# Order of the long and short products in the gate and up units, and the place of one norm's spread

## The chip, the cores and the metric

The kernel runs on one core of one Trainium2 chip. The metric is the device time of one execution in microseconds; the time before is the median of three runs. TensorE (PE) multiplies, VectorE (DVE) and ScalarE (ACT) split the weights and empty PSUM, GpSimd (POOL) does small side work, and SyncE (SP) issues the transfers.

## The reference

256 tokens of width 1024 go through two layers. Each has a half-step SwiGLU block, a mixer (a Mamba-2 scan in the first layer, sliding-window attention in the second) and a second half-step SwiGLU block; a final norm ends it. All is float32. A SwiGLU block, of which there are four, is the part that the change touches:

```
def swiglu(h, w_gate, w_up, w_down):
    return (jax.nn.silu(h @ w_gate) * (h @ w_up)) @ w_down
x = x + FFN_RES_WEIGHT * swiglu(rmsnorm(x, norm_w[layer, 0]), ffn_w_gate[layer, 0], ffn_w_up[layer, 0], ffn_w_down[layer, 0])
```

The inner width is 2816, which is 22 tiles of 128.

## The kernel before

Weights come as units of 128 by 1024, in the order of a list that the program fixes. A unit is split into a rounded part `hi` (ACT, L145) and the rest `lo` (DVE, L156), four units ahead of its use (`ahead`). The activations are split in the same way into `xh` and `xl`, which lie side by side in a tile `xs` of 512 columns for each of the eight slices k of the width. A product of two split numbers needs three of the four parts: hi times xh, hi times xl, lo times xh.

The four SwiGLU blocks have the keys f0 to f3. For each tile f of the inner width a block has a gate unit g, an up unit u and, from f = 4 on, a down unit d of the tile four earlier. The last down units follow at the block's end.

A gate or up unit (`wide`, L357) has 16 matmuls into one PSUM bank: eight **long products** of 512 columns (hi times xs, which is xh and xl at once) and eight **short products** of 256 columns (lo times xh, into the bank's first half). With f = 0 long and short ones alternate, since the activations of slice k become ready one by one. With f > 0 all eight long products come first and then all eight short ones. A down unit (`rows`, L379) has 24 matmuls of 256 columns. After the products ACT copies the bank's second half and DVE adds the first half (`add`, L516).

The normalizing factor of a block is not applied to the input but to the results. `rs_slots` (L418) spreads this work over the units: `h0` sums the squares on PE (L312), and after it DVE and POOL take the root; `h1` builds a diagonal matrix on DVE (L332); `h2`, the **spread**, multiplies it on PE (L337), and ACT copies the factors `rs` out (L339). What may run behind a unit stands in a table of slots, one slot for each unit; `tick` runs it when the unit's matmuls have been issued. In f0 `h0` stands in slot 3, `h1` in slot 4 and `h2` in slot 5, which is behind the up unit of f = 2. In the other blocks they stand in slots 0, 1 and 2, so that `h2` is behind the gate unit of f = 1.

When `rs` is there, `evac` turns g and u of a tile into the split operand of the down unit in three steps, one slot apart: e0 scales (L494, L496) and applies silu, e1 multiplies (L499) and rounds to `hh`, e2 takes the rest `hl` (L503). In f0 the results of the first tiles wait for `rs`; the line that holds them back is

```
wait = max(0, 5 - f) if key == "f0" else 2 if f == 0 else 0
```

Each engine runs its instructions in the order in which the program issues them.

Of the kernel before, what the change touches and what calls it, by code (L numbers as in the profile page):

```python
# [18 lines left out]
D = 1024  # L19
KT = D // P  # L20
# [10 lines left out]
DI = 2048  # L31
HEADS = 32
GROUPS = 4
# [183 lines left out]
class Trunk:  # L217
# [138 lines left out]
            before()  # L356
        self.tick()  # L357

    def wide(self, what, out, by_part=False):


        hi, lo = self.W.next(what)
        passes = [(k, w, x, n) for k in range(KT) for w, x, n in ((hi, self.xs, 2 * T), (lo, self.xh, T))]
        if by_part:
            passes = passes[0::2] + passes[1::2]
        for n, (k, w, x, c) in enumerate(passes):
            self.nc.tensor.matmul(  # L367
                out[:, 0:c], w[:, k * P : (k + 1) * P], x[k],
                start=n == 0, stop=n == len(passes) - 1, skip_group_check=True,
            )  # L370
        self.tick()
# [43 lines left out]

        return done

    def rs_slots(self, acc, n, key, d, got, quick=False):  # L418

        st = {}  # L420

        def h0():
            st["b"], st["y"] = self.rs_stats(acc(), n, key)

        def h1():
            st["dg"] = self.rs_diag(st["y"], key)

        def h2():
            got(self.rs_spread(st["b"], st["dg"], key), st["y"])

        self.slots.late(d, h0)
        self.slots.at(d + 1, h1)
        self.slots.late(d + (1 if quick else 2), h2)

    def last_stage(self):
        nc = self.nc
# [38 lines left out]
    def stage_norm(self, key):  # L475
        def got(rs, y):
            self.rs, self.rtok = rs, y

        self.rs_slots(lambda: self.sq_parts, D, key, 3 if key == "f0" else 0, got)


    def ffn(self, l, i, key, nxt):
        nc, wk = self.nc, self.fw
        self.stage_norm(key)
        accs = self.accs(f"da_{key}")
        hs = {}

        def evac(f, g, u):
            hh = self.op.tile([P, T], F32R, tag="high", name=f"hh_{key}_{f}")
            hl = self.op.tile([P, T], F32R, tag="low", name=f"hl_{key}_{f}")  # L490
            hs[f] = (hh, hl)

            def e0():
                nc.vector.tensor_tensor(g, g, self.rs, ALU.mult)  # L494
                nc.scalar.activation(g, g, AF.Silu)
                nc.vector.tensor_tensor(u, u, self.rs, ALU.mult)  # L496

            def e1():
                nc.vector.tensor_tensor(u, u, g, ALU.mult)  # L499
                nc.scalar.activation(hh, u, AF.Copy)  # L500

            def e2():
                nc.vector.tensor_tensor(hl, u, hh.bitcast(F32), ALU.subtract)  # L503

            wait = max(0, 5 - f) if key == "f0" else 2 if f == 0 else 0
            self.slots.chain(wait, [e0, e1, e2])

        def product(name, f, t):

            b = self.bank(f"{name}_{key}_{f}")  # L510
            if self.W.pos == 0:
                self.slots.at(0, lambda: nc.scalar.copy(t, b[:, 0:T]))
                self.unit((name, l, i, f), b[:, 0:T])
                return

            def add():  # L516
                nc.scalar.copy(t, b[:, T:])  # L517
                nc.vector.tensor_tensor(t, b[:, 0:T], t, ALU.add)  # L518

            self.slots.at(0, add)  # L520
            self.wide((name, l, i, f), b, by_part=f > 0)

        for f in range(NF):
            g, u = (wk.tile([P, T], F32, tag=n, bufs=4, name=f"{n}s_{key}_{f}") for n in "gu")
            product("g", f, g)
            evac_now = lambda: evac(f, g, u)
            self.slots.late(0, evac_now)
            product("u", f, u)
            if l == 1 and i == 0 and f == 0:
                self.split_k()  # L530
            if l == 1 and i == 0 and f == 5:
                self.shared_k()
            if f >= LAG:
                self.down(l, i, f - LAG, hs, accs)
        for f in range(NF - LAG, NF - TAIL):
            self.down(l, i, f, hs, accs)
        self.tail([(("d", l, i, f), *hs.pop(f)) for f in range(NF - TAIL, NF)], accs, nxt)
# [15 lines left out]
    def ssm(self, nxt):  # L553
# [19 lines left out]
        yh, yl, sq, R = {}, {}, {}, {}  # L573
# [92 lines left out]
        def csb(hg):  # L666
            t = wk.tile([P, 4, 3 * P], F32, tag="csb", bufs=2, name=f"csb{hg}")
            nc.sync.dma_start(t, scratch[4 * hg : 4 * hg + 4, :].unsqueeze(0).broadcast_to([P, 4, 3 * P]))
            CSB[hg] = t

        def cb(g):
            b = side(f"cb{g}")
            nc.tensor.matmul(b[:, 0:T], B[g][:, 0:P], C[g], start=True, stop=True)
            nc.tensor.matmul(b[:, T : T + P], B[g][:, P:T], C[g][:, P:T], start=True, stop=True)

            def e():
                m = wk.tile([P, 3, P], F32, tag="cbm", name=f"cbm{g}")
                V.tensor_tensor(m[:, 0], b[:, 0:P], causal, ALU.mult)
                V.tensor_tensor(m[:, 2], b[:, T : T + P], causal, ALU.mult)
                A.copy(m[:, 1], b[:, P:T])  # L680
                CB[g] = m

            sl.at(1, e)
# [22 lines left out]
        def prep(g):  # L706

            es = [wk.tile([P, 2, 3, P], F32, tag="E", bufs=6, name=f"E{4 * g + n}") for n in range(4)]

            def p0(n):  # L710
                tok = st["tok"]
                for i in range(2):
                    h = 8 * g + 2 * n + i
                    row = CSB[h // 4][:, h % 4]
                    A.activation(es[n][:, i, 0:2], row[:, 0:T], AF.Relu, bias=tok[:, 0, h : h + 1])
                    if i == 0:
                        V.tensor_scalar(es[n][:, i, 2], row[:, T:], tok[:, 1, h : h + 1], 0.0, ALU.add, ALU.max)
                    else:
                        A.activation(es[n][:, i, 2], row[:, T:], AF.Relu, bias=tok[:, 1, h : h + 1])

            def p1():
                for e in es:
                    A.activation(e, e, AF.Exp, scale=-1.0)  # L723

            def p2(n):
                f = es[n].rearrange("p n b l -> p n (b l)")
                c = CB[g].rearrange("p b l -> p (b l)").unsqueeze(1).broadcast_to([P, 2, 3 * P])
                V.tensor_tensor(f, f, c, ALU.mult)  # L728
                M[4 * g + n] = es[n]

            sl.chain(0, [lambda: p0(0), lambda: p0(1), lambda: p0(2), lambda: p0(3), p1])
            for n in range(4):
                sl.at(5 + n + DECAY_AT[g], lambda n=n: p2(n))
# [24 lines left out]
        def scale(g):  # L758
            for tt in range(4 * g, 4 * g + 4):
                V.tensor_tensor(ys[tt], ys[tt], R[g], ALU.mult)  # L760
# [36 lines left out]
        for hg in range(8):  # L797
            g = hg // 2
# [5 lines left out]
        for g in range(GROUPS):  # L804
            plan(E["C", g] + 3 + SLACK, lambda g=g: cb(g))
            sl.at(base + start[g] - sl.now, lambda g=g: prep(g))
            for hg in (2 * g, 2 * g + 1):
                y = ymm_at[hg]
                plan(turned[hg], lambda hg=hg: xtok(hg))
                plan(start[g] - 2 + 2 * (hg % 2), lambda hg=hg: csb(hg))  # L810
                plan(y, lambda hg=hg: ymm(hg))
            last = max(max(ymm_at[t // 2] + 1, E["z", t] + 2) for t in range(4 * g, 4 * g + 4))

            def got(rs, y, g=g):
                R[g] = rs

            def norm(g=g, got=got):
                self.rs_slots(lambda: sq[g], DI // GROUPS, f"yg{g}", 0, got, True)

            plan(last + 1 + NORM_AT[g], norm)  # L820
            done = last + 3 + NORM_AT[g] + SCALE_AT[g]
            sl.at(base + done - sl.now, lambda g=g: scale(g))
            for tt in range(4 * g, 4 * g + 4):
                n = min(at["so", tt], NIN - TAIL) - 3
                if n < done:
                    n = min(at["so", tt], NIN - TAIL) - 2
                assert n >= done, (tt, n, done)
                sl.at(base + n - sl.now, lambda tt=tt: ysplit(tt))
# [414 lines left out]
```

## Time and profile before

| | |
|---|---|
| median of three runs | 1035.71 us (1035.37, 1035.71, 2038.25) |
| the profiled execution's own time | 1036.34 us |
| its span | 1034.5 us |
| mean granted TensorE clock | 0.997 |
| PE busy | 1014.0 us, 98% of the span |
| DVE busy | 780.1 us, 75% |
| ACT busy | 627.9 us, 61% |
| POOL busy | 80.4 us, 8% |

One run of the three took 2038.25 us, twice the others; the median stands beside the two that agree. The span is counted from the first to the last instruction, and 1.8 us of the profiled execution's time lie around it. The busy time of PE is an envelope: matmuls overlap in the pipeline, each shows 0.28 or 0.39 us, and the distance between two starts is shorter. Distances between starts are what is read below.

### The profile page before, as it was taken

What the parts mean: (1) busy time and instruction counts of PE and PEld (TensorE: products, weight loads), DVE (VectorE), ACT (ScalarE), POOL (GpSimd) and SP (SyncE); (2) the same over time, 40 slices, a digit from 0 to 9 for tenths busy, and PEclk for the clock granted to TensorE, in tenths of its full rate; (3) what the DMA queues carried; (4) which work ended last, traced back from release to release, by engine and by line L of the source; (5) the groups of instructions that cost most, each with busy time, mean ns of one, the idle gap of its engine ahead of it and who ended that gap; (6) DMA issues with size and microseconds to landing.
All of it is one profiled execution on the core that took longest, in us unless ns stands there. A gap on an engine that the chain in (4) does not pass through costs nothing.

```text
span 1034.5 us, 18344 instructions
## 1 busy us (share of the span) xinstructions
PE 1014.0 (98%) x7290; PEld 940.7 (91%) x7290; DVE 780.1 (75%) x1418; ACT 627.9 (61%) x1106; POOL 80.4 (8%) x124
## 2 busy tenths in 40 slices
PE   9999999999999999999999999999999999999996
PEld 8899999999989898999999899999998898999996
DVE  5866666889999978766667896666689877666665
ACT  7555555669886756555555664555565775555554
POOL 3000000210111112000000200000022020000000
PEclk9999999999999999999999999999999999999998
DMA  8555554556546354555555465555545335555531
GB/s 327 206 182 201 192 195 180 176 188 264 184 150 225 132 194 173 190 196 204 173 202 202 157 208 206 171 203 197 199 175 161 117 132 201 187 180 204 188 118 41
DMA packets 29845, 190.85 MB, mean 184 GB/s; under 512 B 3744, under 2 KB 5312, under 8 KB 8256
## 3 DMA queue, kind: packets, MB, share of 16 engines
q1 hardware_dynamic: 29328, 188.90, 51.3%
q8 instruction: 57, 0.93, 0.4%
q10 hardware_dynamic: 432, 0.79, 0.2%
q14 instruction: 28, 0.23, 0.1%
HBM read 187.27 MB, written 1.10 MB: 182 GB/s over the span
## 4 chain that ended last, share of the span: by engine, by line
PE 82%; DVE 9%; ACT 4%; DMA 2%; POOL 2%; issue 1%; POOLq 0%; SPq 0%
PE da_f L387 23%; PE u_f L367 23%; PE g_f L367 23%; PE sa L387 4%; PE sb L354 3%; DVE lo L156 2%; DMA csb<-cs_scratch 2%; PE aa L387 2%; PE q L354 1%; DVE xs L606 1%; ACT hi L145 1%; DVE E L728 1%; ACT E L723 1%; PE kab L354 1%; DMA X<-x 1%
## 5 line engine op out<-in xcount | busy, mean ns | idle before, releaser
L156 DVE TENSOR_TENSOR lo<-raw,hi 128x1024 fp32r<-128x1024 f32 (+1 forms) x343 | 414.7, 1213 | 11.7 <-ACT hi L145 11.7
L145 ACT ACTIVATE hi<-raw 128x1024 fp32r<-128x1024 f32 (+1 forms) x343 | 356.8, 1047 | 10.3 <-PE sa L387 4.3
L387 PE MATMUL da_f<-hh_f,lo 128*128 128x256 f32 x704 | 195.0, 277 | 0.0
L387 PE MATMUL da_f<-hh_f,hi 128*128 128x256 f32 x704 | 194.9, 277 | 0.0
L387 PE MATMUL da_f<-hl_f,hi 128*128 128x256 f32 x704 | 194.9, 277 | 0.0
L367 PE MATMUL u_f<-xs,hi 128*128 128x512 f32 x704 | 179.9, 393 | 0.0
L367 PE MATMUL g_f<-xs,hi 128*128 128x512 f32 x696 | 176.9, 393 | 0.3 <-DVE xs L399 0.3
L367 PEld LDWEIGHTS u_f<-xs,hi 128*128 128x128 f32 x704 | 126.5, 188 | 22.2
L367 PEld LDWEIGHTS g_f<-xs,hi 128*128 128x128 f32 x696 | 124.6, 188 | 23.3 <-DVE xs L399 1.1
L387 PEld LDWEIGHTS da_f<-hl_f,hi 128*128 128x128 f32 x704 | 132.2, 188 | 0.0
L387 PEld LDWEIGHTS da_f<-hh_f,lo 128*128 128x128 f32 x704 | 132.2, 188 | 0.0
L387 PEld LDWEIGHTS da_f<-hh_f,hi 128*128 128x128 f32 x704 | 132.0, 188 | 0.0
L518 DVE TENSOR_TENSOR gs_f<-g_f,gs_f 128x256 f32<-128x256 f32 x87 | 36.9, 424 | 107.8 <-ACT gs_f L517 107.6
L367 PEld LDWEIGHTS u_f<-xs,lo 128*128 128x128 f32 x704 | 95.3, 188 | 7.1
L367 PEld LDWEIGHTS g_f<-xs,lo 128*128 128x128 f32 x696 | 95.0, 188 | 6.8
L518 DVE TENSOR_TENSOR us_f<-u_f,us_f 128x256 f32<-128x256 f32 x88 | 37.3, 424 | 84.0 <-ACT us_f L517 83.9
L367 PE MATMUL u_f<-xs,lo 128*128 128x256 f32 x704 | 99.7, 277 | 0.0
L367 PE MATMUL g_f<-xs,lo 128*128 128x256 f32 x696 | 99.0, 279 | 0.0
L517 ACT COPY us_f<-u_f 128x256 f32<-128x256 f32 x88 | 32.6, 371 | 106.0 <-PE u_f L367 105.9
L354 PE MATMUL sb<-xs,hi 128*128 128x256 f32 x656 | 86.8, 282 | 0.0
L517 ACT COPY gs_f<-g_f 128x256 f32<-128x256 f32 x87 | 32.1, 369 | 83.1 <-PE g_f L367 83.1
L354 PEld LDWEIGHTS sb<-xs,hi 128*128 128x128 f32 x656 | 80.8, 188 | 0.9 <-issue 0.5
(267 smaller groups left out, 1303.7 us busy)
## 6 DMA issues: line engine op xcount, KB each, us to landing
raw<-w SPq DMA_DIRECT2D x168, 1024.0 KB, 4.9
csb<-cs_scratch SPq DMA_DIRECT2D x8, 768.0 KB, 6.8
raw<-w SPq DMA_DIRECT2D x4, 512.0 KB, 6.8
Q<-r_q SPq DMA_DIRECT2D x32, 32.0 KB, 1.9
out<-o SPq DMA_DIRECT2D x3, 256.0 KB, 2.1
ca<-const_att SPq DMA_DIRECT2D x1, 704.0 KB, 6.3
X<-x SPq DMA_DIRECT2D x2, 256.0 KB, 5.9
first_x<-x SPq DMA_DIRECT2D x1, 288.0 KB, 4.4
```

The costliest lines, as they stand in the source:

```text
L145: self.nc.scalar.activation(hi[:, s], self.chunks[c][:, i, s], AF.Copy)
L156: self.nc.vector.tensor_tensor(lo[:, s], self.chunks[c][:, i, s], hi[:, s].bitcast(F32), ALU.subtract)
L354: nc.tensor.matmul(out, w[:, k * P : (k + 1) * P], x[k], start=n == 0, stop=n == len(passes) - 1)
L367: self.nc.tensor.matmul(out[:, 0:c], w[:, k * P : (k + 1) * P], x[k], start=n == 0, stop=n == len(passes) - 1, skip_group_check=True,)
L387: nc.tensor.matmul(out, w[:, s], x, start=f and j < 4 and m == 0, stop=e and m == 2, skip_group_check=True)
L517: nc.scalar.copy(t, b[:, T:])
L518: nc.vector.tensor_tensor(t, b[:, 0:T], t, ALU.add)
L606: V.scalar_tensor_tensor(out, u[:, tap : tap + T], self.s("convw", tap * 24 + c), out, ALU.mult, ALU.add)
L723: A.activation(e, e, AF.Exp, scale=-1.0)
L728: V.tensor_tensor(f, f, c, ALU.mult)
```

## The change

Three things change. In gate units with f > 0 the eight short products come first and the eight long ones after them. In up units with f > 0 one short product comes first, then the eight long ones, then the other seven short ones. In f0 the spread moves from slot 5 to slot 6, behind the gate unit of f = 3, and the steps of `evac` that wait for it move one slot with it. In the scan's four group norms the argument `True` becomes the gap 1, which is what it meant. No instruction is added or removed.

```diff
-    def wide(self, what, out, by_part=False):
+    def wide(self, what, out, shorts=None):
         hi, lo = self.W.next(what)
         passes = [(k, w, x, n) for k in range(KT) for w, x, n in ((hi, self.xs, 2 * T), (lo, self.xh, T))]
-        if by_part:
-            passes = passes[0::2] + passes[1::2]
+        if shorts is not None:
+            long, short = passes[0::2], passes[1::2]
+            passes = short[:shorts] + long + short[shorts:]
...
-    def rs_slots(self, acc, n, key, d, got, quick=False):
+    def rs_slots(self, acc, n, key, d, got, gap=2):
...
-        self.slots.late(d + (1 if quick else 2), h2)
+        self.slots.late(d + gap, h2)
...
-        self.rs_slots(lambda: self.sq_parts, D, key, 3 if key == "f0" else 0, got)
+        self.rs_slots(lambda: self.sq_parts, D, key, *((3, got, 3) if key == "f0" else (0, got)))
...
-            wait = max(0, 5 - f) if key == "f0" else 2 if f == 0 else 0
+            wait = max(0, 6 - f) if key == "f0" else 2 if f == 0 else 0
...
-            self.wide((name, l, i, f), b, by_part=f > 0)
+            self.wide((name, l, i, f), b, shorts=None if f == 0 else KT if name == "g" else 1)
```

Lines behind the head of `wide` have a number higher by one in the new kernel.

PE, where the gate unit of f = 9 in f0 ends and its up unit begins, before (`xs` with `hi` is a long product, with `lo` a short one):

```order
L367 MATMUL g_f_9_901<-xs_90,lo_807 128x256
L367 MATMUL g_f_9_901<-xs_91,lo_807 128x256
L367 MATMUL u_f_9_927<-xs_84,hi_811 128x512
L367 MATMUL u_f_9_927<-xs_85,hi_811 128x512
L367 MATMUL u_f_9_927<-xs_86,hi_811 128x512
```

The same place in the change:

```order
L368 MATMUL g_f_9_901<-xs_90,hi_779 128x512
L368 MATMUL g_f_9_901<-xs_91,hi_779 128x512
L368 MATMUL u_f_9_927<-xs_84,lo_835 128x256
L368 MATMUL u_f_9_927<-xs_84,hi_811 128x512
L368 MATMUL u_f_9_927<-xs_85,hi_811 128x512
```

The two long groups now lie next to each other, with one short product between them; the gate's short group lies against the down unit before it, and the up unit's last seven against the down unit behind it.

PE, at the spread of f0, before:

```order
L367 MATMUL u_f_2_360<-xs_90,lo_260 128x256
L367 MATMUL u_f_2_360<-xs_91,lo_260 128x256
L337 MATMUL st_f_310<-dg_f_351,ones 128x256
L367 MATMUL g_f_3_392<-xs_84,hi_264 128x512
L367 MATMUL g_f_3_392<-xs_85,hi_264 128x512
```

and in the change:

```order
L368 MATMUL g_f_3_389<-xs_90,hi_264 128x512
L368 MATMUL g_f_3_389<-xs_91,hi_264 128x512
L337 MATMUL st_f_310<-dg_f_351,ones 128x256
L368 MATMUL u_f_3_415<-xs_84,lo_326 128x256
L368 MATMUL u_f_3_415<-xs_84,hi_289 128x512
```

The spread now stands one unit later, behind a gate unit.

DVE, around the rest `hl` of tile 0, which the first down unit of f0 reads, before:

```order
L518 TENSOR_TENSOR us_f_3_391<-u_f_3_418,us_f_3_391 128x256
L156 TENSOR_TENSOR lo_444<-raw_196,hi_416 128x1024
L503 TENSOR_TENSOR hl_f_0_259<-us_f_0_208,hh_f_0_258 128x256
L499 TENSOR_TENSOR us_f_1_267<-us_f_1_267,gs_f_1_266 128x256
L494 TENSOR_TENSOR gs_f_2_332<-gs_f_2_332,rs_f_380 128x256
```

and in the change:

```order
L519 TENSOR_TENSOR gs_f_4_445<-g_f_4_447,gs_f_4_445 128x256
L156 TENSOR_TENSOR lo_471<-raw_262,hi_443 128x1024
L504 TENSOR_TENSOR hl_f_0_259<-us_f_0_208,hh_f_0_258 128x256
L500 TENSOR_TENSOR us_f_1_267<-us_f_1_267,gs_f_1_266 128x256
L495 TENSOR_TENSOR gs_f_2_332<-gs_f_2_332,rs_f_409 128x256
```

`hl` of tile 0 now stands behind the add of the gate unit of f = 4 and not behind that of the up unit of f = 3; the down unit that reads it has kept its place.

## Rows read from the trace of the kernel before

**Rows 1.** Page, part 1: busy time, share of the span, instructions.

```profile
PE 1014.0 (98%) x7290; PEld 940.7 (91%) x7290; DVE 780.1 (75%) x1418; ACT 627.9 (61%) x1106; POOL 80.4 (8%) x124
```

**Rows 2.** Waits of PE, whole span: total us, times, longest.

```profile
PE st_yg L337 <- DVE dg_yg L332: 5.4, 4, 2.0
...
PE st_f L337 <- DVE dg_f L332: 0.5, 1, 0.5
```

**Rows 3.** Timeline, PE, one tile of f0: start, duration, what, count.

```profile
58.91 2.00 PE L367 MATMUL g_f<-xs,hi 128*128 128x512 f32 x8
60.75 1.07 PE L367 MATMUL g_f<-xs,lo 128*128 128x256 f32 x8
61.65 1.99 PE L367 MATMUL u_f<-xs,hi 128*128 128x512 f32 x8
63.48 1.11 PE L367 MATMUL u_f<-xs,lo 128*128 128x256 f32 x8
64.43 0.28 PE L387 MATMUL da_f<-hh_f,hi 128*128 128x256 f32 x1
```

**Rows 4.** Timeline, PE, one tile of f1.

```profile
424.29 1.99 PE L367 MATMUL g_f<-xs,hi 128*128 128x512 f32 x8
426.12 1.11 PE L367 MATMUL g_f<-xs,lo 128*128 128x256 f32 x8
427.06 2.00 PE L367 MATMUL u_f<-xs,hi 128*128 128x512 f32 x8
428.89 1.07 PE L367 MATMUL u_f<-xs,lo 128*128 128x256 f32 x8
429.80 0.28 PE L387 MATMUL da_f<-hh_f,hi 128*128 128x256 f32 x1
```

**Rows 5.** Timeline, PE: first of 120 down products and what follows, f0 and f1.

```profile
181.19 0.28 PE L387 MATMUL da_f<-hh_f,hi 128*128 128x256 f32 x1
...
195.32 0.28 PE L354 MATMUL sb<-xs,hi 128*128 128x256 f32 x1
...
561.53 0.28 PE L387 MATMUL da_f<-hh_f,hi 128*128 128x256 f32 x1
...
575.13 0.39 PE L367 MATMUL g_f<-xs,hi 128*128 128x512 f32 x1
```

**Rows 6.** Timeline, PE, f1, groups of f = 2 and 3 behind the spread.

```profile
405.01 2.00 PE L367 MATMUL g_f<-xs,hi 128*128 128x512 f32 x8
406.86 1.11 PE L367 MATMUL g_f<-xs,lo 128*128 128x256 f32 x8
407.80 2.00 PE L367 MATMUL u_f<-xs,hi 128*128 128x512 f32 x8
409.63 1.07 PE L367 MATMUL u_f<-xs,lo 128*128 128x256 f32 x8
```

**Rows 7.** Timeline, PE, f0, alternating products of the first up unit.

```profile
12.87 0.39 PE L367 MATMUL u_f<-xs,hi 128*128 128x512 f32 x1
13.10 0.28 PE L367 MATMUL u_f<-xs,lo 128*128 128x256 f32 x1
13.22 0.40 PE L367 MATMUL u_f<-xs,hi 128*128 128x512 f32 x1
```

**Rows 8.** Timeline, all engines, the spread of f0, idle time and releaser in brackets.

```profile
27.25 0.48 DVE L332 TENSOR_SCALAR dg_f<-co,y_f 128x128 f32<-128x128 f32 x2 [1.71 <-POOL y_f L325]
...
27.78 0.70 PE L337 MATMUL st_f<-dg_f,ones 128*128 128x256 f32 x2 [0.51 <-DVE dg_f L332]
```

**Rows 9.** Timeline, the rest of tile 0 on DVE and its first reader on PE.

```profile
36.18 0.42 DVE L503 TENSOR_TENSOR hl_f<-us_f,hh_f 128x256 fp32r<-128x256 f32 x1
...
39.52 0.28 PE L387 MATMUL da_f<-hl_f,hi 128*128 128x256 f32 x1
```

**Rows 10.** Timeline, the lower part of the second up unit and that unit's start.

```profile
16.19 1.29 DVE L156 TENSOR_TENSOR lo<-raw,hi 128x1024 fp32r<-128x1024 f32 x1 [2.03 <-ACT hi L145]
...
17.77 0.39 PE L367 MATMUL u_f<-xs,hi 128*128 128x512 f32 x1
```

More of the change, by code (lines that the diff above doesn't have):

```diff
@@ L817, in norm @@
             def norm(g=g, got=got):
-                self.rs_slots(lambda: sq[g], DI // GROUPS, f"yg{g}", 0, got, True)
+                self.rs_slots(lambda: sq[g], DI // GROUPS, f"yg{g}", 0, got, 1)
             plan(last + 1 + NORM_AT[g], norm)
```

## The prediction

> **What bounds the kernel.** I read the shares of busy time first: PE has something in flight for 98% of the span, DVE for 75% [rows 1]. Then the waits of PE: the four spreads of the scan take 5.4 us together, that of f0 0.5 us, and each other group 1.1 us at most; all ten of them come to 11 us of 1034.5 [rows 2]. So the sequence of matmuls sets the time. No other engine can give much, and a reordering can only pay if the same matmuls follow each other faster. I therefore looked in the timeline of PE at the distances between starts, group by group.
>
> One tile of f0 shows it [rows 3]. The gate's eight long products last from 58.91 to 60.75, 1.84 us, its eight short ones 0.90; the up unit's eight long ones 1.83, its short ones 0.95. The short products differ, though shape and operands are alike: 0.90 for the gate, 0.95 for the up unit. In f1 it is the other way round, 0.94 for the gate and 0.91 for up [rows 4]. The down products behind the up unit keep the pace of its short ones. A stretch of 120 of them gives it most sharply: 14.13 us in f0, which is 117.8 ns each, and 13.60 us in f1, 113.3 ns each [rows 5]. So a short product has a **loose** pace and a **tight** one, 4.4 ns apart, and it keeps the pace until a long group comes. A group of eight long products changes it: behind loose ones it ends in tight ones, behind tight ones in loose ones. In the four blocks 82 long groups start behind loose products and end in tight ones, and 74 the other way round. Two groups per tile flip it twice, so a block keeps the foot on which it starts: f0 has its down products loose, f1 to f3 tight.
>
> The exceptions matter. In f1 the gate group at 405.01, the second long group behind the spread, lasts 1.85 us, starts behind loose products and ends in loose ones, 0.94; the next one, 407.80 to 409.63, flips [rows 6]. There are five such groups in the trace.
>
> **The change, part by part.** Nothing is added or removed, so PE, DVE and ACT keep their instructions and the DMA queues their transfers. Five edits remain.
>
> 1. *Order within a tile.* Today 8 short products lie between the two long groups and 32 between tiles. Then 1 lies between the groups and 39 between tiles. If one short product is enough to part two flips, only that one runs loose and 39 run tight. A tile in the steady state: eight short gate products 0.907 (8 x 113.3 ns), long group 1.83, one loose short product 0.118, long group 1.84, seven tight ones 0.793, 24 down products 2.720.
>  - f0: its 22 down units change pace, 528 x 4.4 ns = 2.3 us. Its up units from f = 3 on, 19, go from 0.943 (eight loose) to 0.118 + 0.793 = 0.911: 0.6 us. Its gate groups are tight already. Together **2.9 us**.
>  - f1 to f3: the down products are tight already. 57 gate groups go from 0.943 to 0.907, 2.1 us; 57 up groups from 0.907 to 0.911, -0.2 us. Together **1.9 us**.
>  - The long groups keep their two lengths, 1.83 and 1.84, and only change places: nothing.
>  The first tiles of a block, up to f = 2, and the place in f2 where two key units stand in between have their own pattern before and after; I put them at nothing, and at 0.3 us either way for the range.
>
> 2. *Price of the single short product.* No row shows one between two groups of eight. The nearest are the alternating products of f0's first up unit: a single short product takes 0.12 us (13.10 to 13.22), the long one before it 0.23 [rows 7]. So it costs 0.113 to 0.124 us by itself; I take the loose pace, 0.118. What it does to the next long group those rows don't tell, since there a long product never follows a long one. That is the open point of this case.
>
> 3. *`lo` is wanted at the start of a unit, not in its middle.* It is made four units ahead. The tightest place is the second up unit: its `lo` is done at 16.19 + 1.29 = 17.48, and the unit starts at 17.77 [rows 10]. The new order wants it then and not 1.8 us later; 0.29 us are left, so nothing. If that cover goes, the wait is as long as `lo` is late.
>
> 4. *The spread of f0.* Today PE stands for 0.51 us because the diagonal starts on DVE only at 27.25 [rows 8]. One unit later it has been ready for 2 us: **0.5 us** saved. The copy of `rs` is then late by one unit, and with it the whole chain on DVE. Queued behind it there are the adds and the `lo` parts, but these have units to spare. The first down unit has not: `hl` of tile 0 ends at 36.60, and its reader starts at 39.52 [rows 9]. From the spread to that end it takes 36.60 - 27.78 = 8.82 us. The new spread comes after 27.27 (no wait) plus one gate unit of 2.76: 30.03. So `hl` ends at about 38.85, and its reader is due at 39.52 - 0.51 = 39.01. 0.16 us remain: nothing, or up to 0.4 us if DVE is held up once more.
>
> 5. *The results leave PSUM as before*: the copy waits for a unit's last product in either order, and a unit has the same 16.
>
> The sum: 2.9 + 1.9 + 0.5 = 5.3 us off the profiled execution's 1036.34, which is 1031.0. That execution is 0.6 us above the median of 1035.71, and a median is what will be measured, so the forecast is 1035.7 - 5.3 = **1030.4**. Its own range is 1029.6 to 1031.7: 0.3 us down and 0.3 + 0.4 + 0.6 up, for what I put at nothing and for the base. The rivals too are given against the median.
>
> [...] The same shape runs at 113.3 and at 117.8 ns, by what ran before it [rows 5]. [...]
>
> **The rivals.**
>
> *Order is worth nothing.* If the pace depends on the block and not on the order, only edit 4 counts: 1035.7 - 0.5 = 1035.2. Against it: gate and up have opposite paces in the same block, and swap them between f0 and f1 [rows 3, 4]. Chance 0.1.
>
> *Flips, but on the wrong foot.* Two flips per tile keep what the block starts with. If the products behind the spread leave the 39 loose and the one tight: the down products of f1 to f3, 3 x 528 x 4.4 ns = 7.0 us, their 57 up groups 0.030 each = 1.7, the gate groups of f0 19 x 0.037 = 0.7, less 0.5: +8.9, **1044.6**. For it: in f1 the first groups behind the spread are loose for three units before the pattern settles [rows 6]. Against it: it settles on the tight foot in three blocks whose spread stands behind a gate unit, where f0's will stand too. Chance 0.15.
>
> *No flip behind a single product: slower than before.* The second of two long groups parted by one short product may be like the one at 405.01, which lasted 1.85 and left the pace loose [rows 6]. Then all 40 short products of a tile are loose and nothing brings the tight pace back: 7.0 for the down products, 57 up groups 2.1, f0's gate groups 0.7, long groups 0.01 each for 152, 1.5, less 0.5: +10.8, **1046.5**. It decides as soon as one loose product does not count as a loose group. For it: all 82 flips had 8 or more short products before them, and the flip has a count of its own, as the five exceptions show. Against it: the exceptions all follow a disturbance of the stream, the spread or foreign units, and behind a lone short product the long ones of [rows 7] last as long as others. Chance 0.2.
>
> *Block by block.* One or two blocks on the wrong foot: each costs about 3.5 us in f1 to f3 (a third of 7.0 + 1.7, and the 0.6 us of its gain), so 1033.9 to 1037.4. Chance 0.05.
>
> **The numbers.** The forecast has 0.5: 82 of 87 long groups behind loose products flipped. The range runs from 1029.6, the lower end of the forecast, to 1047.0. It holds the forecast, the first, second and last rival, together 0.8, and the lower side of the third, whose long groups could cost a little more than the 0.01 us set here. The two signs share most of the chance; the forecast's own range is 1029.6 to 1031.7. About 2% is what a measurement of this kernel is taken to tell from no change; that is 20.7 us. No case reaches that: faster 0.01, within 2% 0.97, slower 0.02 for a wait that I don't see.
>
> **What the changed profile would show.** Right: a tile takes 8.21 us in all four blocks (0.907 + 1.83 + 0.118 + 1.84 + 0.793 + 2.720), before 8.34 in f0 and 8.23 in f1; 120 down products at a block's end last 13.6 us in f0 too; the spread of f0 has no wait on DVE; `hl` of tile 0 ends before its reader is due. Wrong: 14.1 us for the 120 in any of f1 to f3 tells of the wrong foot or of no flip. Which of the two, the single short product and the long group behind it tell: with the flip the 39 follow a group of 1.83, without it both long groups leave 118 ns behind them.

## The result, and the profile after

The change took 1044.93 us, median of five runs (1037.92, 1041.96, 1044.93, 1045.0, 1046.38), beside 1035.93 for the kernel before on the same chip: a ratio of 1.0067, 95% interval 1.0054 to 1.0081. The forecast was 1030.4. Its sign was wrong; the time lies within the range and fits the rival *Flips, but on the wrong foot* (1044.6). The five runs lie 8.5 us apart, those of before 1.5 apart but for the one of 2038 us. That scatter is the first clue.

The profiled execution is the 1037.92 one, with a span of 1036.1 us against 1034.5. PE still bounds it, with the same instructions and 3.9 us more busy time than in [rows 1]. First part 1 of its page, then the waits of PE (total us, times, longest).

```profile
PE 1017.9 (98%) x7290; PEld 944.6 (91%) x7290; DVE 780.6 (75%) x1418; ACT 627.9 (61%) x1106; POOL 80.3 (8%) x124
```

```profile
PE st_yg L337 <- DVE dg_yg L332: 3.4, 3, 1.6
```

The wait for the diagonal of f0, 0.5 us in [rows 2], is gone, and no wait in a block has taken its place. The scan's waits fell from 5.4 to 3.4 us, but that gains little: from 296 to 299 us the granted clock was 0.50, sixteen products there took 3.4 us and not 2.0, and they filled time in which PE had waited before. That is also some 1.5 of the 3.9 us of busy time. From the last down product of f0 to the first gate product of f1 it is 196.8 us, against 197.1 before. The loss is pace, not waiting. Here is the timeline of PE in the change (start, duration, what, count), first a tile of f0, which answers to [rows 3], then one of f1, which answers to [rows 4], and the next one of f1 from its gate's long group on.

```profile
57.92 1.07 PE L368 MATMUL g_f<-xs,lo 128*128 128x256 f32 x8
58.83 1.99 PE L368 MATMUL g_f<-xs,hi 128*128 128x512 f32 x8
60.66 0.28 PE L368 MATMUL u_f<-xs,lo 128*128 128x256 f32 x1
60.77 2.01 PE L368 MATMUL u_f<-xs,hi 128*128 128x512 f32 x8
62.62 0.96 PE L368 MATMUL u_f<-xs,lo 128*128 128x256 f32 x7
...
420.83 1.10 PE L368 MATMUL g_f<-xs,lo 128*128 128x256 f32 x8
421.77 2.00 PE L368 MATMUL g_f<-xs,hi 128*128 128x512 f32 x8
423.61 0.28 PE L368 MATMUL u_f<-xs,lo 128*128 128x256 f32 x1
423.73 2.01 PE L368 MATMUL u_f<-xs,hi 128*128 128x512 f32 x8
425.57 0.99 PE L368 MATMUL u_f<-xs,lo 128*128 128x256 f32 x7
...
430.17 2.00 PE L368 MATMUL g_f<-xs,hi 128*128 128x512 f32 x8
432.00 0.28 PE L368 MATMUL u_f<-xs,lo 128*128 128x256 f32 x1
432.11 1.99 PE L368 MATMUL u_f<-xs,hi 128*128 128x512 f32 x8
433.94 0.99 PE L368 MATMUL u_f<-xs,lo 128*128 128x256 f32 x7
```

In f0 the tile is the one that was forecast: eight short products 0.91 (57.92 to 58.83), the long group 1.83, the single short product 0.12, the long group 1.85. In f1 the same eight short ones take 0.94. Two kinds of tile take turns there. In the first nothing flips: both long groups take 1.84, and the single short product between them is as loose as the others (117 ns). In the second the gate's group flips to tight, the single short product is tight (113 ns), and the up unit's group flips back, so that 39 are loose and one is tight. From the first down product of one tile to that of the next it is 8.213 us in f0; in f1 it is 8.395 (no flip) and 8.371 (two flips) in turn. The down products at the end of each block tell the same; these rows are the first of 120 and what follows them, for f0, f1 and f3, and answer to [rows 5].

```profile
178.40 0.28 PE L388 MATMUL da_f<-hh_f,hi 128*128 128x256 f32 x1
...
192.00 0.28 PE L354 MATMUL sb<-xs,hi 128*128 128x256 f32 x1
...
560.53 0.28 PE L388 MATMUL da_f<-hh_f,hi 128*128 128x256 f32 x1
...
574.66 0.40 PE L368 MATMUL g_f<-xs,hi 128*128 128x512 f32 x1
...
1011.44 0.28 PE L388 MATMUL da_f<-hh_f,hi 128*128 128x256 f32 x1
...
1025.05 0.38 PE L457 MATMUL fin<-last_sq,ones 128*128 128x256 f32 x1
```

13.60 us in f0, 14.13 in f1, 13.61 in f3: f0 and f3 run on the tight foot, f1 and f2 on the loose one. Before, f0 was the loose block and the other three were tight. From a block's first down product to its last, before and after:

| | f0 | f1 | f2 | f3 | sum |
|---|---|---|---|---|---|
| before | 155.80 | 153.45 | 159.33 | 153.45 | 622.04 |
| change | 153.29 | 156.54 | 162.30 | 153.11 | 625.24 |

So f0 gained 2.5 us, f3 0.3, and f1 and f2 lost 3.1 and 3.0: a sum of +3.2 us. The rest of the execution, the spread of f0 among it, gave back 1.6; the spans differ by 1.6.

Where do the blocks part? In their first tiles, around the spread. Timeline of PE in the change, the gate's long group before the spread and what follows, of f1 (a block that came out loose) and of f3 (tight):

```profile
396.28 2.01 PE L368 MATMUL g_f<-xs,hi 128*128 128x512 f32 x8
398.13 0.59 PE L337 MATMUL st_f<-dg_f,ones 128*128 128x256 f32 x2
398.37 0.47 PE L368 MATMUL u_f<-xs,lo 128*128 128x256 f32 x1
398.68 2.00 PE L368 MATMUL u_f<-xs,hi 128*128 128x512 f32 x8
400.52 0.99 PE L368 MATMUL u_f<-xs,lo 128*128 128x256 f32 x7
...
850.31 2.00 PE L368 MATMUL g_f<-xs,hi 128*128 128x512 f32 x8
852.15 0.59 PE L337 MATMUL st_f<-dg_f,ones 128*128 128x256 f32 x2
852.39 0.47 PE L368 MATMUL u_f<-xs,lo 128*128 128x256 f32 x1
852.71 2.00 PE L368 MATMUL u_f<-xs,hi 128*128 128x512 f32 x8
854.54 0.96 PE L368 MATMUL u_f<-xs,lo 128*128 128x256 f32 x7
```

The instructions are the same. The short product behind the spread takes 0.31 us in f1 and 0.32 in f3 (306 and 313 ns in the trace's own starts), and the seven behind the long group come out loose in the one and tight in the other, 0.82 and 0.79 us to the next unit. But they differed before the spread: the long group ahead of it takes 1.85 us in f1 and 1.84 in f3, behind eight short products that are loose in both. In the trace's own starts it is 1.851 or 1.852 in all seven loose blocks and 1.838 or 1.839 in all four tight ones, wherever the spread stands behind a gate unit of the new order (the two profiles of the change and that of the order alone, both below). Further ahead lies the block's first tile, whose alternating products wait for slices of the activations one by one; that these waits make the difference is not shown.

The two rows that answer to [rows 8, 9], of the timeline of all engines:

```profile
29.92 0.59 PE L337 MATMUL st_f<-dg_f,ones 128*128 128x256 f32 x2
...
38.16 0.42 DVE L504 TENSOR_TENSOR hl_f<-us_f,hh_f 128x256 fp32r<-128x256 f32 x1
...
38.72 0.30 PE L388 MATMUL da_f<-hl_f,hi 128*128 128x256 f32 x1
```

The spread has no idle time before it. `hl` of tile 0 ends at 38.58; its reader starts 0.14 us later and, at 138 ns behind its predecessor, some 0.02 late. That small wait turns the foot: the rest of this down unit is loose (118 ns), and so are the next tile's gate products (0.94); behind that tile's long groups the products are tight again. In the second profile of the same program the same product comes 140 ns behind its predecessor, and the products stay tight.

### The profile page after: what moved, and what is told of

Read it like the earlier page. It is cut to its first block, busy times and chain, and to the rows that moved or that the text cites. A ratio compares the mean times of both kernels' runs of the same rounds, so it can differ in the third digit from the quotient of the medians.

```text
span 1036.1 us, 18364 instructions
## 1 busy us (share of the span) xinstructions
PE 1017.9 (98%) x7290; PEld 944.6 (91%) x7290; DVE 780.6 (75%) x1418; ACT 627.9 (61%) x1106; POOL 80.3 (8%) x124
## 4 chain that ended last, share of the span: by engine, by line
PE 84%; DVE 9%; ACT 3%; DMA 2%; POOL 1%; issue 1%; POOLq 0%; SPq 0%
PE da_f L388 24%; PE u_f L368 24%; PE g_f L368 23%; PE sa L388 4%; PE sb L354 3%; DVE lo L156 2%; DMA csb<-cs_scratch 2%; PE aa L388 1%; PE q L354 1%; DVE xs L607 1%; DVE E L729 1%; ACT E L724 1%; PE kab L354 1%; DMA X<-x 1%; DVE S L941 1%
## 5 line engine op out<-in xcount | busy, mean ns | idle before, releaser
L368 PE MATMUL u_f<-xs,lo 128*128 128x256 f32 x704 | 114.9, 280 | 0.0
L368 PEld LDWEIGHTS u_f<-xs,lo 128*128 128x128 f32 x704 | 101.9, 188 | 10.4
L368 PEld LDWEIGHTS g_f<-xs,lo 128*128 128x128 f32 x696 | 88.4, 188 | 0.3
```

What stands on the lines that cost most here:

```text
L368: self.nc.tensor.matmul(out[:, 0:c], w[:, k * P : (k + 1) * P], x[k], start=n == 0, stop=n == len(passes) - 1, skip_group_check=True,)
```

## The experiments

The theory after the result: the time goes with the number of blocks on the loose foot (a foot that repeats from tile to tile is also called a course); the order of before comes back to the tight foot after a disturbance, the new order keeps whatever it starts with. Rivals: the foot is fixed by the program; a single short product never parts two flips; the time was lost elsewhere. Every kernel below differs from the change or from another kernel by the lines shown. All times and ratios stand against the kernel before on the same chip: 1037.02 us beside the first four kernels (the two of one part, the two of the switch at f = 4), 1036.1 beside the late switch and two, five and four short products, 1036.18 beside the rest.

**One part each.** The spread moved, the order of before:

```diff
-            self.wide((name, l, i, f), b, shorts=None if f == 0 else KT if name == "g" else 1)
+            self.wide((name, l, i, f), b, shorts=None if f == 0 else 0)
```

> Old order of long and short products in all tiles, only the spread of f0 moved behind the gate unit of f = 3. Theory A (the pace is a state that a block takes on at its start and keeps; the new order has a tight and a loose cycle, the old one only a small difference between its two): f0 now starts as f1 to f3 do, its 22 down units become tight, 2.3 us, and the wait of 0.5 us goes: 1035.9 - 2.8 = 1033.1, all runs within 1 us of each other. Rival B (the moved spread is what disturbs the kernel, by the later factors): 1036 or more, with runs several us apart.

And the new order with the spread in its old place:

```diff
-        self.rs_slots(lambda: self.sq_parts, D, key, *((3, got, 3) if key == "f0" else (0, got)))
+        self.rs_slots(lambda: self.sq_parts, D, key, 3 if key == "f0" else 0, got)
...
-            wait = max(0, 6 - f) if key == "f0" else 2 if f == 0 else 0
+            wait = max(0, 5 - f) if key == "f0" else 2 if f == 0 else 0
```

> New order of products in all four blocks, the spread of f0 in its old slot. Theory A: each block still falls on a tight or a loose foot, about 3.5 us per loose block from 1031: 1031.5 to 1046, several us between runs. Rival B (the moved spread is the cause): about 1031, runs within 1 us.

The spread alone: 1032.86 us (1032.6 to 1034.67, four of the five within 0.4 us), ratio 0.9967, interval 0.9954 to 0.998. The order alone: 1046.01 (1043.25 to 1048.54), 1.0089, 1.0074 to 1.0105; its median is at the upper end of what theory A expected, and its slowest runs lie above. So the whole loss is the order's, and the spread gains 4.2 us, eight times its wait. The rows of the first kernel behind the spread of f0 show where the larger part comes from (timeline of PE):

```profile
29.94 0.59 PE L337 MATMUL st_f<-dg_f,ones 128*128 128x256 f32 x2
...
32.21 1.10 PE L368 MATMUL u_f<-xs,lo 128*128 128x256 f32 x8
...
35.00 1.11 PE L368 MATMUL g_f<-xs,lo 128*128 128x256 f32 x8
...
37.77 1.07 PE L368 MATMUL u_f<-xs,lo 128*128 128x256 f32 x8
```

Two groups behind the spread stay loose (0.95 and 0.94 us for eight short products), the third turns tight. With an up unit next to the spread the third is an up unit, and the down products behind it are tight. Before, a gate unit stood there. In f1 to f3 of the same kernel the three groups are tight, loose, tight (0.91, 0.94, 0.91): another start, and the same foot from the third on. All four blocks of this kernel are tight: 120 down products take 13.60 or 13.61 us in each, and a tile 8.233. From first to last down product f0 takes 153.45 us and not 155.80; that is 2.35 of the 3.7 us between the two profiles' spans. Another 0.7 lie ahead of its first down product, the wait of 0.5 among them, and the rest is spread over the other stages. In the profile of the order alone f1 is tight (8.213) and the other three are loose: not the pair of the change.

**Where the switch comes.** The order of before in a block's first tiles, the new one from f = 4 on:

```diff
-            self.wide((name, l, i, f), b, shorts=None if f == 0 else KT if name == "g" else 1)
+            self.wide((name, l, i, f), b, shorts=None if f == 0 else 0 if f < 4 else KT if name == "g" else 1)
```

> As the change, but f = 1 to 3 of each block keep the old order (long group, then short group); the new order starts at f = 4. Theory A: the three old tiles put every block on the tight foot before the new order starts, and it keeps it: 1030.4, between 1029.6 and 1031.5 in every run; tiles of 8.21 us in all four blocks. Rival C (the new order loses its foot by itself in the course of a block): 1034 to 1046, several us between runs.

1037.61 us (1033.9 to 1039.41), ratio 1.0004, interval 0.9991 to 1.0017: the expected time was missed. Its profile has f1 and f3 tight to their end and f0 loose: there the spread stands right before the switch, within the two groups that stay loose. f2 is tight up to the key units and loose behind them (timeline of PE, f2):

```profile
612.92 0.96 PE L368 MATMUL u_f<-xs,lo 128*128 128x256 f32 x7
613.71 1.12 PE L354 MATMUL kab<-xkh,hi 128*128 128x256 f32 x8
...
627.04 0.98 PE L368 MATMUL u_f<-xs,lo 128*128 128x256 f32 x7
...
630.70 1.10 PE L368 MATMUL g_f<-xs,lo 128*128 128x256 f32 x8
```

So the new order holds the tight foot where nothing disturbs it, and in f2 it does not find it again in the sixteen tiles behind the key units. In the next kernel the gate unit of f = 4 too has the old order, so that the new one begins behind a gate unit's short products, which are loose, and not behind tight down products:

```diff
-            self.wide((name, l, i, f), b, shorts=None if f == 0 else KT if name == "g" else 1)
+            self.wide((name, l, i, f), b, shorts=None if f == 0 else 0 if f < 4 + (name == "g") else KT if name == "g" else 1)
```

> As the run with three old tiles, but the gate unit of f = 4 keeps the old order too, so that the switch comes between gate and up and the up unit's single short product follows short ones. Theory A: the blocks enter the new order on the loose foot: 1043 to 1047 in every run, 120 down products at a block's end 14.1 us in all four blocks. Rival C: the same time as the run with three old tiles, to 1 us.

1044.86 us (1044.12 to 1045.91), 1.008, interval 1.0067 to 1.0093; all four blocks loose, at 8.371 and 8.395 us a tile. One unit's place in the switch makes 7 us.

The switch put behind every disturbance:

```diff
-            self.wide((name, l, i, f), b, shorts=None if f == 0 else KT if name == "g" else 1)
+            old = {"f0": 7, "f2": 9}.get(key, 4)
+            self.wide((name, l, i, f), b, shorts=None if f == 0 else 0 if f < old else KT if name == "g" else 1)
```

> The order of before is kept in each block's first tiles (f below 7 in the first block, below 9 in the third, below 4 in the second and fourth), past the spread of factors, the first down units and the key units, and the order of the change runs from there on; the spread is moved as in the change. Theory A (the tight course holds by itself under the new order and is lost only where something disturbs the row of products): the switch comes with the products tight in all four blocks and they stay so, about 1031.5 us (1032.86 of the spread alone less some 65 tiles at 0.02 us), runs within 1.5 us of each other. Rival B (the new order loses the course by itself, after some tiles): loose blocks again, 1036 to 1046, and runs that differ by 3.5 us and its multiples.

1032.74 us (1030.72 to 1033.39), 0.9961, interval 0.9949 to 0.9973. All four blocks are tight and stay so, 8.213 us a tile behind the switch; rival B is out. The six runs lie 2.7 us apart, more than the 1.5 expected and less than one loose block costs (3.4). It beats both kernels. The 1031.5 were not reached: from first to last down product its blocks sum to 618.45 us, against 619.69 with the spread alone, 1.2 us less, where 1.3 were expected; but in its scan the profiled execution took some 1.5 us longer (last section). In total time the two can't be told apart.

**How many short products part the groups.** Three kernels change the last number of the line, 1, to 2, 5 and 4; a fourth sets it to 0.

```diff
-            self.wide((name, l, i, f), b, shorts=None if f == 0 else KT if name == "g" else 1)
+            self.wide((name, l, i, f), b, shorts=None if f == 0 else KT if name == "g" else 2)
```

> Up's two long groups are parted by two short products instead of one; everything else is the change. Theory A (what counts is where a long group's start falls, and the number of short products ahead of it decides that; with one short product two repeating courses exist, 8.21 us a tile and 8.38 us a tile, and a block stays on the one it starts on; with two or with eight the group behind starts on the tight course whatever came before): all four blocks run tight, tile 8.21 us, the 120 down products of every block take 13.6 us, about 1031 us (1030 to 1033), and the runs agree within 1.5 us. Rival B (any parting by fewer than eight short products leaves both courses; the one is as good as two): like the change, 1038 to 1047 with blocks on either course. Rival C (long groups cost the same in any order, and the change lost its time elsewhere): 1045 again, as the change.

> Up's two long groups are parted by five short products; the rest is the change. Theory A (the number of short products counts by its remainder against three, since three long products end where they began in the pattern of starts): five acts as two and eight do, tight in all blocks, 1030 to 1033 us. Rival B (the more short products part the groups the better): between the change and the order of before, 1033 to 1045, and better than with two. Rival C (no parting but eight holds): 1038 to 1047.

> Up's two long groups are parted by four short products; the rest is the change. Theory A (the remainder against three counts): four acts as one does, loose blocks, 1037 to 1047 us. Rival B (the more short products the better): better than with two, 1030 to 1033 us.

> No short product parts up's long group from the gate's: sixteen long products in a row, then up's eight short ones; the rest is the change. Theory A (a turn of the foot comes with each group of eight long products that has short ones ahead of it, and sixteen in a row turn it once): tile by tile the 40 short products are tight and loose in turn, 8.20 and 8.37 us a tile, whatever the block started on, 8.285 on the mean against 8.213: about 1037.5 (1036 to 1039), with runs that agree within 1.5 us. Rival B (sixteen turn it twice): two courses as in the change, all 40 tight or all loose, 1031 to 1046 and runs that differ by 3.5 us and its multiples. Rival C (they leave it loose in any case): 1045 to 1047.

| short products between | median us (runs) | ratio, interval | tile, tight us | tile, loose us | loose blocks in the profile |
|---|---|---|---|---|---|
| 8, spread alone | 1032.86 (5) | 0.9967, 0.9954-0.998 | 8.233 | 8.340 (before, f0) | none |
| 5 | 1040.91 (4) | 1.0047, 1.0031-1.0064 | 8.220 | 8.353 | f1 to f3 |
| 2 | 1041.89 (6) | 1.005, 1.0033-1.0066 | 8.207 | 8.366 | f2, f3 |
| 1, the change | 1044.93 (5) | 1.0067, 1.0054-1.0081 | 8.213 | 8.371, 8.395 in turn | f1, f2 |
| 4 | 1044.32 (4) | 1.0078, 1.0064-1.0091 | none seen | 8.358, 8.395 in turn | all |
| 0 | 1038.41 (10) | 1.0023, 1.0014-1.0033 | 8.228, 8.352 in turn | the same | each half |

My expectation for two and five, that the long group behind them always starts on the tight foot, fell: both have a loose course and stay on it. That four act as one does held, but the remainder against three, from which I had it, is out with the other two. What holds is the count, with two, five and eight. With n short products between the groups, n run on one foot and 40 - n on the other: from 8 to 5 to 2 the tight tile loses 0.013 us a step, three times 4.4 ns, and the loose one gains as much. Fewer products between the groups therefore give little on the tight foot and raise what the loose one costs: 0.107 us a tile with eight, 0.160 with two, 0.170 with one. With four and with one every second loose tile follows the count (8.358, 8.371); the other takes 8.395 with either, since nothing flips in it and all 40 are loose. With none the sixteen long products turn the foot once a tile (timeline of PE, f1):

```profile
428.47 1.07 PE L368 MATMUL u_f<-xs,lo 128*128 128x256 f32 x8
...
436.67 1.10 PE L368 MATMUL u_f<-xs,lo 128*128 128x256 f32 x8
```

The up unit's short ones are tight in one tile (0.91, 428.47 to the first down product at 429.38) and loose in the next (0.94). No block is on one foot, and the runs agree within 2.2 us. On the tight course, then, a single short product between the groups is enough to part two flips.

**Does the order of before find the tight foot, or was it luck?** The kernel with the spread alone, and the spreads of f1 to f3 one unit later, so that a gate unit follows them:

```diff
-        self.rs_slots(lambda: self.sq_parts, D, key, *((3, got, 3) if key == "f0" else (0, got)))
+        self.rs_slots(lambda: self.sq_parts, D, key, *((3, got, 3) if key == "f0" else (0, got, 3 if key[0] == "f" else 2)))
...
-            wait = max(0, 6 - f) if key == "f0" else 2 if f == 0 else 0
+            wait = max(0, 6 - f) if key == "f0" else max(0, 3 - 2 * f)
```

> The order of before in all units, the spread of the first block moved as in the change (behind the gate unit of f = 3), and the spreads of the other three blocks moved one unit later too, so that they stand behind the up unit of f = 1 with a gate unit behind them, as the first block's spread did before. Against the run with the first spread alone moved (1032.86 us against 1037.02 before). Theory A (the kind of unit that follows the spread sets the foot in the order of before: two groups behind it stay loose and the third turns tight, so the down products are tight if an up unit follows and loose if a gate unit follows; the key units in the third block set it anew, to tight): the 120 down products at the end of the second and fourth block take 14.1 us, in the third and first 13.6; 528 down products x 4.4 ns in each of two blocks, 4.7 us, and 0.2 before the key units: about 1037.8, as slow as before. Rival B (the gain of the first block came from its wait, and the other blocks have a tight foot of their own): 13.6 us in all four, 1032.9. Rival C (a spread one unit later is always better): under 1032.

1039.56 us (1039.24 to 1039.97), ratio 1.0039, interval 1.0025 to 1.0052. Timeline of PE: the 120 down products of f1 and of f2 with what follows them, and behind them f2 around the key units, whose 48 products and one down unit end at 621.74.

```profile
561.49 0.28 PE L388 MATMUL da_f<-hh_f,hi 128*128 128x256 f32 x1
...
575.62 0.39 PE L368 MATMUL g_f<-xs,hi 128*128 128x512 f32 x1
...
750.77 0.28 PE L388 MATMUL da_f<-hh_f,hi 128*128 128x256 f32 x1
...
764.37 0.39 PE L354 MATMUL q<-xs,hi 128*128 128x256 f32 x2
```

```profile
612.22 1.11 PE L368 MATMUL u_f<-xs,lo 128*128 128x256 f32 x8
...
621.74 2.00 PE L368 MATMUL g_f<-xs,hi 128*128 128x512 f32 x8
623.58 1.11 PE L368 MATMUL g_f<-xs,lo 128*128 128x256 f32 x8
624.53 2.00 PE L368 MATMUL u_f<-xs,hi 128*128 128x512 f32 x8
626.36 1.07 PE L368 MATMUL u_f<-xs,lo 128*128 128x256 f32 x8
```

f1 is loose (14.13 us), f2 tight at its end (13.60). Ahead of the key units f2's up unit is loose (0.95, 612.22 to 613.17); behind them the gate group stays loose (0.95) and the up unit turns tight (0.91, 626.36 to the first down product at 627.27). f0 ends tight in 13.60, f3 loose in 14.13. That is theory A, block by block. The blocks sum to 624.47 us, 4.8 more than with the spread alone, as expected; the median is 1.8 us above what was expected, and the profiled execution lost 1.6 in the scan, at the place that the last section shows. Which unit follows the disturbance sets the foot under the order of before, in every profile of it; the five runs agree within 0.8 us. One thing is not explained: of the kernel before, two of 14 runs beside this one took 1033.6 us, 2.6 below their median. That is about what f0 on the tight foot would give (2.35), but neither was profiled.

**The same program once more.** No edit.

> The change itself once more, for a second profile of the same program. Theory A (under the new order a block keeps the course on which the units behind its spread happen to start, and that differs between executions): other blocks are loose than in the first profile, where the second and third were; the time goes with their number, about 1031 plus 3.5 us for each: 1034.5, 1038, 1041.5 or 1045. Rival B (the program fixes the course of each block): the second and third loose again, 1037.9.

One execution, 1041.55 us. f0 is tight (13.60), f1, f2 and f3 are loose (14.13 each). Timeline of PE, the last 120 down products of f3 and what follows:

```profile
1014.54 0.28 PE L388 MATMUL da_f<-hh_f,hi 128*128 128x256 f32 x1
...
1028.67 0.38 PE L457 MATMUL fin<-last_sq,ones 128*128 128x256 f32 x1
```

In the first profile the same block took 13.61: f3 has changed its foot, and three loose blocks were to give 1041.5. The program does not fix the foot of a block; rival B is out. Nor is it a matter of the chip alone: the runs with two short products lie 5.0 us apart on one chip.

## Why the prediction went wrong, step by step

*Edit 1, the order.* The tile was right: 8.213 us on the tight foot, 0.12 for the single short product, 39 products tight. So was "a block keeps the foot on which it starts". The step that failed is the choice of foot, in the words of the rival: "it settles on the tight foot in three blocks whose spread stands behind a gate unit". I read that as a property of the place. It belongs to the order of before: with eight short products between the groups, the kind of unit behind the disturbance decides the foot (the kernel with the later spreads), whichever of two starts the disturbance left. The new order has no return that can be counted on: in its first tiles a block takes the foot that a difference of some 13 ns in one long group goes with, and keeps it while nothing disturbs it; a disturbance may turn it either way, as the late `hl` of f0 and the key units of f2 show. In the sum the place of the error is the first tiles of a block, "I put them at nothing": what happens there costs 3.4 us for a block that comes out loose. The count of 82 of 87 flips, on which the forecast had its 0.5, spoke of whether groups flip, which they do, and not of where the sequence starts. The rows given for the rival were misread in a detail: two units behind the spread are loose, not three [rows 6]. And the lower end of the forecast's own range, 1029.6, does not follow from its terms: 0.3 us down from 1030.4 is 1030.1.

*Its price* was about right: "about 3.5 us" for each block on the wrong foot. From the tight 153.11 to the loose 156.54 it is 3.4 in f1 and f3. In the profiled executions two loose blocks gave 1037.92, three 1041.55, four, in the kernel with the gate unit later, 1044.54. The median run of 1044.93 has no profile; four loose blocks there, as the rival *Flips, but on the wrong foot* had it, fit its time and are not shown.

*Edit 2* was within its bounds. The open point, what the single product does to the next long group, has two answers: on the tight course the pair flips twice, around a single product of 120 ns; on the loose one a tile with two flips and a tile with none take turns. *No flip behind a single product* is out as a rule, since f0 and f3 flip behind one, but it describes every second tile of a loose block. The sign that was to tell the two rivals apart therefore pointed to both; and on the tight course the 39 follow the longer group, 1.85, not the one of 1.83.

*Edit 3* held: no wait of PE for a `lo` appeared.

*Edit 4* held for the wait (0.5 us gone, `hl` 0.02 late), but its larger effect was missed: moving the spread past one unit changes which unit follows it. Alone, under the order of before, the move is worth 4.2 us in the median, of which the pace of f0 is 2.35.

*Edit 5* held. *Order is worth nothing* is out: order alone moved the median by 9 us. The Trainium skill (TensorE: Matmul & The Clock Gate, Back-to-back issue gap) gives the distance of two matmuls by their columns and the weight load beside them, with no term for order. These runs disagree: the same 256 columns go at 113.3 or 117.8 ns by what ran before.

What stays open is what, ahead of the spread, makes the long group 1.84 or 1.85, why the one leads to the tight foot and the other to the loose one, and by what rule the loose course has one tile with two, five and eight products between the groups and two tiles with one and four. The runs show both, not their cause.

## What to carry to other kernels

Where matmuls of two sizes follow each other without gaps, the same product may have two paces and a sequence may keep the one it starts on: read the distances between starts group by group. Before a new order is priced at its better pace, ask what brings it back there after each wait or foreign unit; the order that costs 0.02 us more a tile but returns by itself was the better one here. Runs of one kernel that lie several us apart are a reason to profile it twice.

## What else the runs showed of the hardware

In 7 of the 13 profiles of this case the granted clock fell in the scan behind the wait for the third group's diagonal. These are windows of the kernel with the late switch and of that with the spread alone (window, its length, busy time of PE, PEld, DVE, ACT, POOL, granted clock, DMA share, GB/s).

```profile
339.00:344.00 5.00, 4.84 (x26) 4.79 (x27) 4.93 (x11) 4.98 (x9) 0.00 (x0) 0.66 0.22 48
```

```profile
339.30:344.00 4.70, 4.48 (x36) 4.43 (x37) 4.63 (x11) 4.68 (x9) 0.00 (x0) 1.00 0.17 35
```

Before it PE had waited 1.83 us in the one and 2.00 in the other, so the wait's length alone does not decide. In the first, these products went at the lower level (1.2 GHz), 0.21 us from start to start:

```profile
341.34 0.41 PE L388 MATMUL sa<-yl,hi 128*128 128x256 f32 x1
341.56 0.41 PE L388 MATMUL sa<-yh,lo 128*128 128x256 f32 x1
```

15 of them at 213 and not 118 ns are 1.4 us, which came in some profiles and not in others: not in either profile of the change, nor in that of before. In seven profiles, both of the change among them, the clock fell ahead of the second group's diagonal as well. There it costs nothing: from the first group's spread to the second's it is 21.1 us in all 13. Compare stages, then, and not totals, where a difference is of that size.
